# Splitting one layer's ConvFFN weights ahead of time, during the attention layer before it

## The chip, the cores and the metric

The kernel runs on one core of a Trainium2 chip, in one launch. The metric is the device time of that launch in microseconds (us). The names used below are those of the profile: PE (TensorE matmuls), PEld (its weight loads), DVE (VectorE), ACT (ScalarE), POOL (GpSimd), SP (SyncE, which issues the DMAs).

## What is computed

One step of a decoder trunk of two layers, on 1,024 prompt tokens and 8 sample tokens (1,032 columns, model width 1,024), everything in float32. Layer 0 is *even*: its mixer is windowed attention beside an RWKV-7 recurrence, joined by an output projection. Layer 1 is *odd* (gated spatial mixing). Each layer ends in a ConvFFN of width 2,816, which is the part that the change is about:

```python
def conv_ffn(xn, conv_state, w_gate, w_up, conv_w, conv_b, w_down):
    ...
    gpre = xn @ w_gate
    ext = jnp.concatenate([conv_state.astype(gpre.dtype), gpre], axis=1)
    conv = conv_b + conv_w[CONV_W - 1] * ext[:, CONV_W - 1:CONV_W - 1 + t]
    ...
    h = jax.nn.gelu(conv, approximate=True) * (xn @ w_up)
```

followed by `h @ w_down`, a norm and the residual.

## The kernel before

**Products in three passes.** TensorE multiplies in a format with fewer mantissa bits than float32. So each operand is split into a high part (the value rounded to that format) and a low part (what is left), and a product is three matmuls: high by high (L290), high by low (L291), low by high (L292). `split` (L285 to L287) makes the two parts: ACT copies the high one (L286), then POOL or DVE subtracts it from the source (L287).

**Weights.** Weights come in slabs of 128 output columns, 1,024 rows deep. A list `order` holds all uses in the order of the program; `wget` (L274) hands out the next, and before that calls `wload` (L229) for the slabs up to a look-ahead: 1 slab in the even layer, 3 in the ConvFFN's plain part (`LOOK`, `LOOK2`). `wload` treats a slab as two halves of 128 x 512 (256 KB). A half that is seen for the first time is loaded raw (L260) and split; if the same slab is used again later, its two parts are also stored to DRAM (`wk`, L264), and every later use loads those two parts (L255, twice 256 KB) and splits nothing. Gate and up slabs of the ConvFFN (names that begin with `ga` or `up`) are left out of that: each use loads them raw and splits them anew. All these DMAs are issued on SP.

**The even layer (layer 0)** works on four chunks of tokens (256, 256, 256, 264). For each chunk c, proj(c) runs 20 slabs `win_even` and out(c) runs 8 slabs `wout_even`; in between stands core(c), attention and the RWKV chunk recurrence, with many short dependent steps. The stages come in the order proj(0), proj(1), proj(2), out(0), proj(3), out(1), out(2), out(3). In the trace proj(2), out(0), proj(3) and most of out(1) lie between 236 and 600 us. A projection's columns that RWKV needs pass through `lerp` (L914): the last column of the chunk before is copied into `zm` by POOL (L927), ACT fills the rest (L928), POOL copies the new last column into `carry` (L930), and DVE mixes (L931). Slabs of the even layer accumulate in two PSUM banks called `le`.

**The sample tokens** go through their own chain in the even layer: `attn_sample` (from L1156; its first ACT step after the scores is L1189), then `rwkv_sample` (from L1225): some small matmuls, two transposes (L1269), a trip of the rows through DRAM, four rounds on the matrix state (L1292 to L1302, POOL and DVE), a second trip through DRAM, and the transpose L1311. After it the ConvFFN's operand tiles `xA` are filled and its first slabs run.

**A small ring.** `stile` (L141) hands out tiles from a ring of four buffers, tag `s`. Norm inputs, residuals, the sample chain's tiles (`Vc`, `st`, `pr`, `spT`, `stmp`, `rows`, `S`, `St`) and the ConvFFN's input loads `xl` (L522) all come from it, so whoever asks for a tile waits for the release of the one four requests back.

**The first ConvFFN.** Its tokens are two halves, A (512) and B (520). Ten columns of blocks f = 0 to 9 are *plain*: gate slab f and up slab f, first for A, then for B (20 slabs, each used twice: 80 half-slab loads and 80 splits). out(2) and out(3) of the even layer still run in between A's first slabs. Then 12 blocks follow in pairs with a seven-product scheme, whose token combinations DVE prepares (L589 to L620) while B starts; then `w_down`. In the trace A starts at about 718 us, B at about 880 to 910, and the pairs at about 1001.

The scheduler fixes each engine's order when the program is built; on the chip an engine runs its list in that order and waits where an operand isn't ready.

Of the kernel before, what the change touches and what calls it, by code (L numbers as in the profile page):

```python
# [10 lines left out]
F32R = mybir.dt.float32r  # L11
# [5 lines left out]
P = 128  # L17
# [106 lines left out]
def trunk(ctx: ExitStack, tc: tile.TileContext, A, O):  # L124
    nc = tc.nc
    PE, ACT, DVE, POOL, SP = nc.tensor, nc.scalar, nc.vector, nc.gpsimd, nc.sync
# [10 lines left out]
    def nm(s):  # L137
        uid[0] += 1
        return f"{s}_{uid[0]}"
# [18 lines left out]
    def dram(shape, s, dt=F32):  # L158
        return dp.tile(shape, dt, tag=s, name=s)
# [17 lines left out]
    order = []  # L177
# [19 lines left out]
    wcount, wmore, wkept = [0], [], {}  # L197
    wfirst = next(i for i, o in enumerate(order) if o[0] == "gate0")

    def wtile(late):  # L200
        if late:
            wcount[0] += 1
        if late and (wcount[0] <= 4 * W2ONLY or wcount[0] % (NW + FBUFS["w2"]) >= NW):
            return wmore[0]("w2", 512, F32R)
        return wp.tile([P, 512], F32R, tag="w", name=nm("w"))
# [3 lines left out]
    def wfactor(name, f, i):  # L209

        if i == 0:
            wraw[name, f] = [stile("wa")[:, 0:512] for _ in range(4)]
            for k, t in enumerate(wraw[name, f]):
                SP.dma_start(out=t, in_=A[name][f + k // 2][:, k % 2 * 512:k % 2 * 512 + 512])
        r = wraw[name, f]
        if i == 0:
            return r[0]
        if i == 1:
            r.append(stile("ws", "g")[:, 0:512])
            DVE.tensor_tensor(out=r[4], in0=r[2], in1=r[3], op=ALU.add)  # L220
            return r[4]
        if i == 2:
            DVE.tensor_tensor(out=r[4], in0=r[4], in1=r[0], op=ALU.subtract)
            return r[4]
        if i == 3:
            return r[1]
        if i == 4:
            DVE.tensor_tensor(out=r[2], in0=r[0], in1=r[2], op=ALU.subtract)
            return r[2]  # L229
        if i == 5:  # L230
            DVE.tensor_tensor(out=r[4], in0=r[1], in1=r[4], op=ALU.subtract)
            return r[4]
        return r[3]

    def wload(i):

        late = i >= wfirst
        if late:  # L240
            look[0] = LOOK3 if len(order[i]) == 3 else LOOK2
        if len(order[i]) == 3:
            hi, lo = wtile(late), wtile(late)
            split(wfactor(*order[i]), hi, lo, POOL)
            wtiles[i] = tuple([x[:, k * P:(k + 1) * P] for k in range(4)] for x in (hi, lo))
            return
        name, m = order[i]
        again = name[:2] not in ("ga", "up") and order.index((name, m)) < i
        more = name[:2] not in ("ga", "up") and order.count((name, m)) > 1
        hi, lo = [], []  # L250
        for j in range(2):
            t = [wtile(late) for _ in range(2)]
            if again:
                for part in range(2):
                    SP.dma_start(out=t[part].bitcast(F32), in_=wkept[name, m, j, part])  # L255
                hi.append(t[0])
                lo.append(t[1])
                continue
            raw = wp.tile([P, 512], F32, tag="raw", name=nm("raw"), bufs=NRAW)
            SP.dma_start(out=raw, in_=A[name][m][:, j * 512:j * 512 + 512])  # L260
            split(raw, *t, DVE if SW[0] <= i - wfirst < SW[1] and i % SW[2] == 0 or i < SW[3] else POOL)
            for part in range(2 if more else 0):
                kept = wkept[name, m, j, part] = dram([P, 512], nm("wk"))
                SP.dma_start(out=kept, in_=t[part].bitcast(F32))  # L264
            hi.append(t[0])
            lo.append(t[1])
        wtiles[i] = ([hi[k // 4][:, (k % 4) * P:(k % 4 + 1) * P] for k in range(KD)],
                     [lo[k // 4][:, (k % 4) * P:(k % 4 + 1) * P] for k in range(KD)])

    wpos = [0]  # L270

    def soon():

# [2 lines left out]
    def wget(*key):  # L276
        i = wpos[0]
        wpos[0] += 1
        assert order[i] == key, (order[i], key)
        while wnext[0] <= min(i + look[0], len(order) - 1):  # L280
            wload(wnext[0])
            wnext[0] += 1
        return wtiles.pop(i)

    def split(src, hi, lo, eng=None):  # L285
        ACT.activation(out=hi, in_=src, func=AF.Copy)  # L286
        (eng or DVE).tensor_tensor(out=lo, in0=src, in1=hi.bitcast(F32), op=ALU.subtract)  # L287
# [528 lines left out]
def even_layer(env, bnd):  # L816
    g = NSpace(env)
    tc, nc, A, O = g.tc, g.nc, g.A, g.O
    PE, ACT, DVE, POOL, SP = g.PE, g.ACT, g.DVE, g.POOL, g.SP
    SE = [DVE if x == 'd' else POOL for x in SENG]  # L820
    bank, C, V, stile = g.bank, g.C, g.V, g.stile
# [8 lines left out]
    def et(s, n, dt=F32):  # L830
        return (eb if s in LASTING else ec).tile([P, n], dt, tag=s, name=g.nm(s), bufs=EB.get(s, 1))

    def pt_(s):
        return et("p", 528)


    lora = const.tile([P, 512], F32, tag="lora", name="lora")
# [988 lines left out]
```

## Time and profile before

| what | value |
|---|---|
| time, three runs | 2580.53, 2581.8 (median), 2583.38 us |
| the profiled execution | 2581.03 us; its span, first to last instruction, 2579.3 us |
| mean granted TensorE clock | 0.968 of full speed |
| PE, DVE, ACT, POOL busy | 95%, 65%, 39%, 36% of the span |
| HBM | 341.34 MB read, 153.64 MB written, 192 GB/s over the span |
| POOL, splits of weights (L287, 300 of `raw`) | 427.2 us |
| ACT, high parts of weights (L286, 320 of `raw`) | 199.2 us |

PE is the engine with the most work, so a change pays where PE idles, or where it runs at a lower granted clock after idling. The table's busy shares are means over stages with different limits; what matters here are two stretches, the even layer's third and fourth chunk (236 to 600 us, and on to 718) and the up phase of the first ConvFFN (718 to 1001 us).

### The profile page before, as it was taken

What the parts mean: (1) busy time and instruction counts of PE and PEld (TensorE: products, weight loads), DVE (VectorE), ACT (ScalarE), POOL (GpSimd) and SP (SyncE); (2) the same over time, 40 slices, a digit from 0 to 9 for tenths busy, and PEclk for the clock granted to TensorE, in tenths of its full rate; (3) what the DMA queues carried; (4) which work ended last, traced back from release to release, by engine and by line L of the source; (5) the groups of instructions that cost most, each with busy time, mean ns of one, the idle gap of its engine ahead of it and who ended that gap; (6) DMA issues with size and microseconds to landing.
All of it is one profiled execution on the core that took longest, in us unless ns stands there. A gap on an engine that the chain in (4) does not pass through costs nothing. (4 is left out here: it accounts for less than half of the span.)

```text
span 2579.3 us, 49838 instructions
## 1 busy us (share of the span) xinstructions
PE 2447.2 (95%) x18460; PEld 2259.5 (88%) x18460; DVE 1670.7 (65%) x3581; ACT 1003.0 (39%) x1979; POOL 939.2 (36%) x981
## 2 busy tenths in 40 slices
PE   6789998999899899999999999999979999999996
PEld 5678988888788799999998888999879999998985
DVE  5776849756874846666455776435896766655556
ACT  4453545434354344444301143343534444441110
POOL 1611113110455645555323253032655555542221
PEclk9999999999799899999999999999989999999998
DMA  8876757765486743323646888465664233254585
GB/s 314 274 240 208 226 179 236 239 221 164 155 272 217 244 152 99 123 83 123 220 148 228 299 280 277 148 234 197 214 210 140 98 105 123 84 208 148 183 290 167
DMA packets 307603, 500.92 MB, mean 194 GB/s; under 512 B 50272, under 2 KB 93856, under 8 KB 307360
## 3 DMA queue, kind: packets, MB, share of 16 engines
q1 hardware_dynamic: 307360, 497.75, 58.3%
q8 instruction: 145, 2.38, 0.4%
q14 instruction: 98, 0.80, 0.1%
HBM read 341.34 MB, written 153.64 MB: 192 GB/s over the span
## 5 line engine op out<-in xcount | busy, mean ns | idle before, releaser
L287 POOL TENSOR_TENSOR w<-raw,w 128x512 fp32r<-128x512 f32 x300 | 427.2, 1432 | 664.5 <-ACT w L286 602.0
L286 ACT ACTIVATE w<-raw 128x512 fp32r<-128x512 f32 x320 | 199.2, 629 | 478.8 <-PE l L291 296.3
L290 PE MATMUL l<-xB,w 128*128 128x256 f32 (+2 forms) x1120 | 320.0, 286 | 17.9 <-DVE gb L589 16.2
L291 PE MATMUL l<-xB,w 128*128 128x256 f32 (+2 forms) x1120 | 320.5, 286 | 5.1 <-DVE xB L287 5.1
L292 PE MATMUL l<-xB,w 128*128 128x256 f32 (+2 forms) x1120 | 320.5, 286 | 0.0
L291 PE MATMUL l<-xA,w 128*128 128x512 f32 (+1 forms) x896 | 305.9, 341 | 0.0
L290 PE MATMUL l<-xA,w 128*128 128x512 f32 (+1 forms) x896 | 304.6, 341 | 0.5 <-DVE ob L1342 0.3
L292 PE MATMUL l<-xA,w 128*128 128x512 f32 (+1 forms) x896 | 304.9, 340 | 0.0
L290 PE MATMUL le<-xs,w 128*128 128x256 f32 (+1 forms) x896 | 269.9, 302 | 25.4 <-ACT w L286 17.9
L292 PE MATMUL le<-xs,w 128*128 128x256 f32 (+1 forms) x896 | 268.1, 300 | 7.4 <-POOL w L287 5.8
L291 PE MATMUL le<-xs,w 128*128 128x256 f32 (+1 forms) x896 | 264.6, 296 | 0.7 <-DVE xs L287 0.7
L290 PEld LDWEIGHTS l<-xB,w 128*128 128x128 f32 x1120 | 214.3, 192 | 18.6 <-DVE gb L589 16.6
L291 PEld LDWEIGHTS l<-xB,w 128*128 128x128 f32 x1120 | 214.6, 192 | 5.5 <-DVE xB L287 5.3
L292 PEld LDWEIGHTS l<-xB,w 128*128 128x128 f32 x1120 | 214.5, 192 | 0.1
L290 PEld LDWEIGHTS le<-xs,w 128*128 128x128 f32 x896 | 177.9, 199 | 38.9 <-ACT w L286 21.2
L287 POOL TENSOR_TENSOR w<-wa,w 128x512 fp32r<-128x512 f32 x112 | 178.1, 1596 | 57.7 <-ACT w L286 57.7
L730 DVE TENSOR_TENSOR yA<-yA,l 128x512 f32<-128x512 f32 x160 | 110.1, 688 | 132.7 <-PE l L292 131.6
L292 PEld LDWEIGHTS le<-xs,w 128*128 128x128 f32 x896 | 177.1, 198 | 15.5 <-POOL w L287 7.4
L290 PEld LDWEIGHTS l<-xA,w 128*128 128x128 f32 x896 | 169.6, 189 | 19.5 <-ACT w L286 0.6
L292 PEld LDWEIGHTS l<-xA,w 128*128 128x128 f32 x896 | 169.6, 189 | 18.9 <-issue 0.2
L291 PEld LDWEIGHTS l<-xA,w 128*128 128x128 f32 x896 | 169.4, 189 | 18.9 <-DVE pp L311 0.3
L291 PEld LDWEIGHTS le<-xs,w 128*128 128x128 f32 x896 | 178.0, 199 | 4.3 <-issue 2.1
(484 smaller groups left out, 6532.7 us busy)
## 6 DMA issues: line engine op xcount, KB each, us to landing
w<-wk SPq DMA_DIRECT2D x496, 256.0 KB, 4.0
wk<-w SPq DMA_DIRECT2D x272, 256.0 KB, 3.7
raw<-in_down_dram SPq DMA_DIRECT2D x88, 256.0 KB, 4.6
ta<-hd SPq DMA_DIRECT2D x36, 512.0 KB, 4.6
raw<-in_gate_dram SPq DMA_DIRECT2D x64, 256.0 KB, 3.1
raw<-in_up_dram SPq DMA_DIRECT2D x64, 256.0 KB, 3.0
hd<-cb SPq DMA_DIRECT2D x28, 516.0 KB, 3.9
hd<-ub SPq DMA_DIRECT2D x28, 516.0 KB, 3.9
```

Of the source, the lines that this page charges most:

```text
L286: ACT.activation(out=hi, in_=src, func=AF.Copy)
L287: (eng or DVE).tensor_tensor(out=lo, in0=src, in1=hi.bitcast(F32), op=ALU.subtract)
L290: PE.matmul(out, wh, xh, start=start, stop=False, **kw)
L291: PE.matmul(out, wh, xl, start=False, stop=False, **kw)
L292: return PE.matmul(out, wl, xh, start=False, stop=stop, **kw)
L730: DVE.tensor_tensor(out=yc, in0=yc, in1=ps[:, :n], op=ALU.add)
```

## The change

The 20 plain slabs of the first ConvFFN are loaded and split once, ahead of time. A generator `ahead` walks over their 40 halves; `wget` advances it by one half at each of the 40 slabs `win_even` of proj(2) and proj(3) (20 each), so that all 40 halves are done by it. For one half: SP loads the raw half into a tile `ar` of the ring `s`; ACT copies the high part into `ah` (one buffer); POOL subtracts in place, so that `ar` then holds the low part; ACT's queue issues the store of the high part and POOL's queue the store of the low part. `wload` finds these halves in `wkept`, so each of the 80 half-slab uses in the first ConvFFN loads two parts (L255's line) and splits nothing. Lines after the inserted ones move by 16 (helpers) or 18 (even layer).

```diff
--- before.py
+++ after.py
@@ -245,8 +245,8 @@
             wtiles[i] = tuple([x[:, k * P:(k + 1) * P] for k in range(4)] for x in (hi, lo))
             return
         name, m = order[i]
-        again = name[:2] not in ("ga", "up") and order.index((name, m)) < i
-        more = name[:2] not in ("ga", "up") and order.count((name, m)) > 1
+        again = (name, m, 0, 0) in wkept
+        more = name[:2] not in ("ga", "up") and not again and order.count((name, m)) > 1
         hi, lo = [], []
         for j in range(2):
             t = [wtile(late) for _ in range(2)]
@@ -267,7 +267,21 @@
         wtiles[i] = ([hi[k // 4][:, (k % 4) * P:(k % 4 + 1) * P] for k in range(KD)],
                      [lo[k // 4][:, (k % 4) * P:(k % 4 + 1) * P] for k in range(KD)])
 
-    wpos = [0]
+    def ahead(keys):
+
+        for name, m in keys:
+            for j in range(2):
+                raw, hi = stile("ar")[:, 0:512], room[0]()
+                SP.dma_start(out=raw, in_=A[name][m][:, j * 512:j * 512 + 512])
+                split(raw, hi.bitcast(F32R), raw.bitcast(F32R), POOL)
+                for part, (eng, t) in enumerate(((ACT, hi), (POOL, raw))):
+                    kept = wkept[name, m, j, part] = dram([P, 512], nm("wk"))
+                    eng.dma_start(out=kept, in_=t)
+                yield
+
+    wpos, room = [0], [None]
+    first_ffn = dict.fromkeys(o for o in order if o[0] in ("gate0", "up0") and len(o) == 2)
+    spare = ahead(first_ffn)
 
     def soon():
 
@@ -280,6 +294,8 @@
         while wnext[0] <= min(i + look[0], len(order) - 1):
             wload(wnext[0])
             wnext[0] += 1
+        if key[0] == "win_even" and i >= order.index(("wout_even", 0)) - 20:
+            next(spare, None)
         return wtiles.pop(i)
 
     def split(src, hi, lo, eng=None):
@@ -832,6 +848,8 @@
 
     def pt_(s):
         return et("p", 528)
+
+    g.room[0] = lambda: et("ah", 512)
 
 
     lora = const.tile([P, 512], F32, tag="lora", name="lora")
```

How the engines' orders move, at three places on which the prediction rests:

POOL, in the fourth chunk's projection (`carry` and `zm` are the copies of `lerp`; the memsets belong to the RWKV chunk). Before:

```order
L930 COPY carry_4413<-zm_4450 128x1
L927 COPY zm_4528<-carry_2438 128x1
L1414 MEMSET uv_3455 64x512
L1413 MEMSET uv_3543 64x512
L930 COPY carry_4413<-zm_4490 128x1
L927 COPY zm_4567<-carry_2438 128x1
L1423 MEMSET iv_3465 64x256
L1424 MEMSET iv_3465 64x16
L1423 MEMSET iv_3561 64x256
L1424 MEMSET iv_3561 64x16
```

Now:

```order
L303 TENSOR_TENSOR ar_4425<-ar_4425,ah_4426 128x512
L948 COPY carry_4413<-zm_4508 128x1
L279 DMA wk_4432<-ar_4425 128x512
L945 COPY zm_4603<-carry_2438 128x1
L1441 MEMSET iv_3465 64x256
L1442 MEMSET iv_3465 64x16
L948 COPY carry_4413<-zm_4555 128x1
L1441 MEMSET iv_3561 64x256
L303 TENSOR_TENSOR ar_4474<-ar_4474,ah_4475 128x512
L1442 MEMSET iv_3561 64x16
L945 COPY zm_4650<-carry_2438 128x1
L279 DMA wk_4481<-ar_4474 128x512
```

Between the copies there now stand a subtraction of a half (`ar<-ar,ah`) and the issue of its store on POOL itself (`DMA wk<-ar`).

ACT, around the sample tokens' first step, `st<-pp` (`y<-le` closes a slab of out(1), `at`, `es`, `pT`, `oa` are attention, `Z`, `nW` the recurrence). Before:

```order
L1107 ACTIVATE qx_8721<-q_7212 64x256 x2
L324 ACTIVATE p_9304<-y_9029 128x512
L1189 ACTIVATE st_7869<-pp_7860 128x64
L1145 ACTIVATE pT_8438<-m_8439 128x512
L1198 ACTIVATE pr_7874,sq_1479_7875<-pr_7874,sq_1479_7875 64x136
L1200 ACTIVATE sq_1479_7875<-vec,sq_1479_7875 64x1
L1404 ACTIVATE bkt_8206<-pr_8201 128x512
L1153 ACTIVATE oa_7831<-m_8445 128x128
L1590 ACTIVATE y_9029<-le_9107 128x256
```

Now:

```order
L302 ACTIVATE ah_8104<-ar_8103 128x512
L1608 ACTIVATE y_9390<-le_9603 128x256
L1499 ACTIVATE Z_8635<-ch_8680 32x256
L279 DMA wk_8108<-ah_8104 128x512
L1505 ACTIVATE nW_8677<-ch_8699 32x8x32
L1163 ACTIVATE pT_9257<-m_9258 128x512
L302 ACTIVATE ah_8148<-ar_8147 128x512
L1522 ACTIVATE Z_8734<-ch_8721 64x512
L1505 ACTIVATE nW_8677<-ch_8700 32x8x32
L279 DMA wk_8152<-ah_8148 128x512
L1171 ACTIVATE oa_8191<-m_9264 128x128
L1608 ACTIVATE y_9390<-le_9637 128x256
L1207 ACTIVATE st_8229<-pp_8220 128x64
```

`st` stood ahead of out(1)'s third `y`; now it follows out(1)'s last one, behind the last two high parts `ah` and their stores.

PE, at the end of the sample tokens' rows (`pp<-cst,smp` is L1269, L1287 after the change; `le<-xs,w` are slabs of the output projection, `ch` the recurrence of the fourth chunk, `m` attention). Before:

```order
L291 MATMUL le_9277<-xs_119,w_9239 128x256
L292 MATMUL le_9277<-xs_117,w_9240 128x256
L1269 MATMUL pp_7987<-cst,smp 128x128
L1506 MATMUL ch_8361<-Z_8374,nW_8317 64x64 x8
L1144 MATMUL m_8740<-cst,at_8717 128x128 x4
L1269 MATMUL pp_7992<-cst,smp 64x128
L1513 MATMUL ch_8385<-uv_8112,bkt_8110 64x64 x8
```

Now:

```order
L1279 MATMUL pp_8343<-stmp_8300,cst 128x32
L1524 MATMUL ch_9027<-Z_9040,nW_8984 64x64 x8
L1287 MATMUL pp_8347<-cst,smp 128x128
L1531 MATMUL ch_9051<-uv_8568,bkt_8566 64x64 x8
L1533 MATMUL ch_9027<-uv_8568,Am_8527 64x64 x4
L1287 MATMUL pp_8352<-cst,smp 64x128
L1533 MATMUL ch_9027<-uv_8568,Am_8527 64x64 x4
L1351 MATMUL ch_9169<-cst,ot_8720 128x128 x4
```

Before, the two transposes stood inside and right behind out(1)'s last slab, with more attention and three more groups of the recurrence still to come; now out(1) and all of the attention lie ahead of them, and only the end of the recurrence and out(2) follow before L1311.

## Rows read from the trace of the kernel before

**Rows 1.** The page's section 1: the span, and each engine's busy time, share of the span and instructions.

```profile
span 2579.3 us, 49838 instructions
PE 2447.2 (95%) x18460; PEld 2259.5 (88%) x18460; DVE 1670.7 (65%) x3581; ACT 1003.0 (39%) x1979; POOL 939.2 (36%) x981
```

**Rows 2.** The table by stretches of the first ConvFFN's A half and the start of its B half. Columns: from:to and length in us; then busy time (and instructions) of PE, PEld, DVE, ACT and POOL; the granted TensorE clock as a share of 2.4 GHz; the mean busy share of the 16 DMA engines; GB/s moved.

```profile
720.00:830.00 110.00, 110.00 (x593) 93.85 (x593) 69.00 (x128) 54.34 (x101) 56.78 (x73) 1.00 0.74 241
830.00:840.00 10.00, 6.39 (x28) 4.84 (x26) 8.75 (x8) 4.70 (x10) 10.00 (x9) 1.00 0.60 206
840.00:850.00 10.00, 9.96 (x33) 8.14 (x34) 6.30 (x16) 3.65 (x6) 5.11 (x5) 0.66 0.41 129
850.00:860.00 10.00, 10.00 (x46) 7.94 (x45) 6.25 (x13) 4.23 (x7) 5.29 (x6) 1.00 0.83 258
860.00:870.00 10.00, 10.00 (x48) 8.20 (x47) 7.46 (x15) 5.15 (x9) 3.26 (x4) 1.00 1.05 371
870.00:880.00 10.00, 10.00 (x85) 10.00 (x85) 10.00 (x15) 5.13 (x10) 7.70 (x3) 1.00 0.83 312
880.00:890.00 10.00, 4.90 (x32) 4.70 (x31) 10.00 (x12) 2.80 (x7) 5.57 (x4) 0.72 0.66 185
890.00:900.00 10.00, 9.46 (x73) 9.25 (x72) 9.14 (x11) 3.39 (x7) 9.96 (x7) 0.94 0.62 204
900.00:910.00 10.00, 2.93 (x13) 2.93 (x14) 8.68 (x15) 2.91 (x7) 2.83 (x2) 0.58 0.83 261
```

**Rows 3.** The view of waits from 720 to 960 us: engine and line that waited, what it waited for, us in total, times, longest.

```profile
PE l L290 <- DVE gb L589: 7.6, 1, 7.6
...
PE l L291 <- DVE xB L287: 5.1, 1, 5.1
...
PE pp L332 <- DVE sq L330: 3.7, 1, 3.7
```

**Rows 4.** The time order of DVE's instructions: start us, duration us, then line, operation, tiles, shapes and count.

```profile
882.33 3.43 DVE L596 TENSOR_TENSOR yB<-t,yB 128x516 fp32r<-128x516 f32 x2
...
888.72 0.68 DVE L620 TENSOR_TENSOR xc<-xc,ub 128x516 f32<-128x516 f32 x1
...
896.44 1.78 DVE L620 TENSOR_TENSOR xc<-xc,ub 128x516 f32<-128x516 f32 x1
...
898.14 0.68 DVE L596 TENSOR_TENSOR yB<-t,yB 128x516 fp32r<-128x516 f32 x1
```

**Rows 5.** The time order of POOL's instructions in the same stretch, in the same columns.

```profile
873.61 11.60 POOL L287 TENSOR_TENSOR w<-raw,w 128x512 fp32r<-128x512 f32 x4
...
894.49 3.18 POOL L287 TENSOR_TENSOR w<-raw,w 128x512 fp32r<-128x512 f32 x2
```

**Rows 6.** Groups by line from 720 to 1000 us (the up phase of the first ConvFFN): the splits of weights. After the count: busy time, mean ns of one, then the idle time before them and what ended it.

```profile
L287 POOL TENSOR_TENSOR w<-raw,w 128x512 fp32r<-128x512 f32 x76 | 115.2, 1522 | 93.8 <-ACT w L286 86.6 <-DMA w<-wk 6.8
...
L286 ACT ACTIVATE w<-raw 128x512 fp32r<-128x512 f32 x77 | 48.3, 629 | 56.5 <-PE l L291 32.5 <-DMA raw<-in_up_dram 9.2 <-DMA raw<-in_gate_dram 8.6
```

**Rows 7.** The table by stretches again (columns as in Rows 2): the even layer's third and fourth chunk, and the stretch around the start of the ConvFFN.

```profile
236.00:600.00 364.00, 350.59 (x3263) 314.85 (x3262) 261.76 (x864) 170.72 (x419) 71.99 (x137) 0.95 0.68 215
700.00:840.00 140.00, 134.93 (x780) 115.76 (x779) 89.93 (x162) 66.63 (x127) 71.68 (x88) 1.00 0.75 248
```

**Rows 8.** DMA issues from 700 to 840 us: tiles, queue, count, KB each, median us from issue to landing.

```profile
raw<-in_up_dram SPq DMA_DIRECT2D x19, 256.0 KB, 3.0
raw<-in_gate_dram SPq DMA_DIRECT2D x19, 256.0 KB, 3.3
```

**Rows 9.** Groups by line from 236 to 600 us, columns as in Rows 6.

```profile
L287 POOL TENSOR_TENSOR w<-raw,w 128x512 fp32r<-128x512 f32 x16 | 21.7, 1359 | 44.8 <-ACT w L286 27.4 <-DMA w<-wk 11.6 <-DMA ivd<-Am 5.6
...
L927 POOL COPY zm<-carry 128x1 f32<-128x1 f32 x26 | 6.3, 241 | 74.8 <-DVE p L931 37.6 <-DVE wd L931 18.0 <-DVE zv L931 12.1
```

**Rows 10.** One line's instructions, L255 (SyncE's loads of kept weight parts) from 236 to 600 us: durations in ns of an issue, least/median/greatest.

```profile
L255 SPq DMA_DIRECT2D w<-wk x184: 319/382/1392, 236.1 to 599.7; - x184
```

**Rows 11.** The page's section 6, the stores of weight parts, in the same columns as Rows 8.

```profile
wk<-w SPq DMA_DIRECT2D x272, 256.0 KB, 3.7
```

**Rows 12.** The time order (columns as in Rows 4) of the sample tokens' chain on ACT, PE, POOL, and PE again.

```profile
589.93 0.21 ACT L1189 ACTIVATE st<-pp 128x64 f32<-128x64 f32 x1
...
639.73 0.27 PE L1269 MATMUL pp<-cst,smp 128*64 128x128 f32 x1
...
656.09 1.26 POOL L1292 TENSOR_TENSOR St<-S,rows 128x512 f32<-128x512 f32 x1 [2.61 <-DMA S<-in_wkv_state_dram]
...
667.65 1.27 POOL L1299 TENSOR_TENSOR S<-S,St 128x512 f32<-128x512 f32 x1
...
697.19 1.28 POOL L1292 TENSOR_TENSOR St<-S,rows 128x512 f32<-128x512 f32 x1 [1.53 <-DVE ov L1302]
...
702.37 1.27 POOL L1299 TENSOR_TENSOR S<-S,St 128x512 f32<-128x512 f32 x1
...
717.82 0.24 PE L1311 MATMUL pp<-cst,orow 32*128 32x32 f32 x1
```

**Rows 13.** The table by stretches (columns as in Rows 2) from the last step ahead of the sample tokens' state rounds to their end.

```profile
640.00:654.00 14.00, 13.18 (x171) 11.18 (x170) 10.86 (x39) 8.98 (x24) 4.26 (x4) 1.00 0.41 119
654.00:690.00 36.00, 28.29 (x240) 24.39 (x239) 33.34 (x83) 13.40 (x35) 15.79 (x12) 0.57 0.43 134
690.00:716.00 26.00, 25.22 (x232) 23.65 (x231) 15.73 (x33) 6.65 (x16) 7.89 (x11) 1.00 0.80 272
```

## The prediction

> **What bounds the kernel now.** The page's table of engines comes first: PE is busy 2447.2 us of a span of 2579.3 [rows 1], so only stretches in which PE stands still, or runs at a lower granted clock, can give anything back. I looked for those in the first ConvFFN, where the splits go away, by the table of stretches [rows 2]. From 720 to 830 us PE is busy 110.00 of 110.00 at full clock: the splits cost nothing there. It idles 3.61 us at 830 to 840, 5.10 at 880 to 890, 0.54 at 890 to 900 and 7.07 at 900 to 910, 16.3 in all. The clock adds to it: at 840 to 850 it is 0.66 and 33 matmuls run where 46 run in the next slice, (46 - 33) / 46 x 10 = 2.8 us; busy time by missing clock gives 4.90 x 0.28 + 9.46 x 0.06 + 2.93 x 0.42 = 3.2 more. The whole stake is 16.3 + 6.0 = 22.3 us.
>
> The view of waits names what ends the idle time: DVE's multiplication of a gate (7.6 us), its split of B's input (5.1), its sum of squares (3.7) [rows 3]. None of the three is a weight. What a weight's split has to do with them is seen in time order. DVE's L620 takes 1.78 us at 896.44 and 0.68 at 888.72, and two L596 take 3.43 at 882.33 where one takes 0.68 at 898.14 [rows 4]; POOL subtracts weight parts from 873.61 to 885.21 and from 894.49 to 897.67, over the slow ones [rows 5]. So POOL's splits slow DVE, which at 870 to 890 is busy 20.00 of 20.00 and holds up B's start.
>
> **The ConvFFN: what goes.** In the up phase POOL spends 115.2 us on 76 subtractions and ACT 48.3 on 77 copies [rows 6]. With the 80 plain ones nearly all of it goes, at most the whole stake of 22.3 us: PE is full elsewhere. Two things stay. DVE still has all the combinations to make; about 1.1 us per slow instruction is what it gets back. And the weights get heavier: a half was one raw load of 256 KB, now it is two. From 700 to 840 us there are 19 + 19 raw loads [rows 8], so 38 x 0.262 = 10.0 MB more on 248 GB/s x 140 us = 34.7 MB [rows 7]. That makes 319 GB/s, and a DMA share of 0.75 x 319 / 248 = 0.96. The best slice shows 371 GB/s at 1.05 [rows 2]. It fits, with no room for a burst, in a stretch where PE loses nothing now. SP has 80 more issues of 0.38 us [rows 10], 31 us over the 283 of the up phase, and hides them. I take **-14** for this part, two thirds of the stake for the fuller transfers, between -22.3 (everything comes back) and 0 (late weights eat what DVE returns).
>
> The Trainium skill ("HBM Reference", section "Specifications (TRN2)") says that a core streaming alone gets about 425 GB/s, more than its paired share of 358. By that figure 319 GB/s would leave a quarter free and this term would be nearer -18; no slice here shows more than 371, so I keep to the row.
>
> **The even layer: what comes.** Forty halves, from about 236 us on. *ACT*: 40 copies of 0.629 us [rows 6] and 40 store issues of about 0.38 [rows 10] are 40 us, beside 170.72 busy of 364 [rows 7]; it hides them. But there is one `ah`: a copy waits on ACT until the store before it has landed, 3.7 us for such a store [rows 11]. Behind it in ACT's order stand the copies that empty the two `le` banks, and PE waits for those. Halves are asked for one per slab, and 364 us / 40 is 9 us apart, more than 0.6 + 0.4 + 3.7 = 4.7, so I cost this at nothing; where halves bunch it is up to 4 us each time. *POOL*: 40 subtractions of 1.36 to 1.52 us [rows 6, 9] are 54 to 61 us. The trace has no DMA issued by POOL; the nearest row is SP's issue, 0.32 to 1.39 us [rows 10], so 13 to 56 us more; I take 15, by the median. POOL is busy 71.99 of 364 and stays below half. The copies into `zm`, 0.24 us each and idle 74.8 us ahead of them now [rows 9], have that much room. *DVE*: 261.76 of 364 busy, 0.72. If each subtraction hits one DVE instruction as above, that is 40 x 1.1 x 0.72 = 32 us of DVE time; PE waits for little of it, as it is busy 350.59 of 364 [rows 7]. *DMA*: 40 x (0.262 read + 0.524 written) = 31.5 MB, 86 GB/s on top of 215, so a share of 0.68 x 301 / 215 = 0.95 with one slab of look-ahead. That is the part that I fear: a slab that lands late stops PE at once. I take **+6** for the layer's body, 0.3 us for each of the 20 slabs of the fuller half of it; the ends are 0 and +32 (all of DVE's loss).
>
> The Trainium skill ("SBUF — State Buffer", section "A bandwidth-pool intuition that's wrong (but worth ruling out)") states that a DMA issued on GpSimd, 620 ns alone, takes 3100 ns beside a DVE copy, since its descriptors wait for DVE. By that rule POOL's 40 stores would take 124 us instead of 15, the ring would give its tiles back later, and I would double the term to +12. No row here shows such a DMA.
>
> **The sample tokens: what is moved.** `ar` comes from the ring of four that the sample chain uses too, and in the new order the chain's first step stands behind the last two halves and behind out(1)'s last slab. Now that step runs at 589.93 us, the last transpose at 639.73, the state rounds from 656.09, and PE takes L1311 at 717.82, with A's first slab right behind it [rows 12]. From transpose to L1311 are 78.1 us. PE's own work in them, at full clock, is 13.18 + 28.29 x 0.57 + 25.22 = 54.5 us [rows 13]. In the new order only what now runs from about 684 us stays behind the transposes: 25.22 and about 3, 28 us. So 54.5 - 28 = 26.5 us of work moves ahead of the chain's slow part, which then runs with less beside it. If the chain takes as long as before, A starts 26.5 us later. It may run faster: the last round, with DVE less loaded, takes 702.37 + 1.27 - 697.19 = 6.5 us to its state, the first 667.65 + 1.27 - 656.09 = 12.8, so three rounds can gain up to 19. I take two thirds of that, **+13**; the ends are +26.5 (nothing gained) and +7.5 (all of it).
>
> **The sum.** -14 + 6 + 13 = +5 on the profiled execution's 2581.0 gives 2586.0; that execution lies 0.8 below the median of 2581.8, so 2586.8, **2587 us**. About 0.2%, 5.2 us, is what a measurement of this kernel can tell from no change: the forecast lies on that edge.
>
> **Rivals.** *Forecast* (0.44): the even layer's costs eat the ConvFFN's gain and a little more; by its own terms from 2579 (18 returned, +2 and +13) to 2599 (14 returned, +6 and +25). For it: the DMA shares of 0.95 and 0.96, and PE's order.
>
> *Faster* (0.38): the sample chain, freed of the competition of attention on DVE, gains back all of the 19 (+7), the early weights land in time (+2), and the ConvFFN returns 18: 2581.8 - 9 = 2573. For it: PE waits for weights hardly anywhere now, POOL is busy a fifth of the time in the even layer, and DVE at 654 to 690 is busy 33.34 of 36.00 [rows 13], the competition that would go. Against it: the chain's four rounds and two trips through DRAM depend on each other.
>
> *Much slower* (0.10): the chain through the ring. If the last halves, waiting for ring tiles, `ah` and stores, come after out(1)'s last slab by their own chain (14 pairs stand back to back on POOL; at 4.7 us a pair that is 66 us), `st` waits with them; if half of the 66 lies behind out(1), A starts 33 us later: 2581.8 + 6 + 33 - 14 = 2607. It decides once the last half's store lands later than out(1)'s end, 638 us now.
>
> *Transfer-bound A half* (0.08): the DMA share reaches 1 in 700 to 840, slabs land late, PE idles at its half clock after. Were 290 GB/s all that it sustains, 319 / 290 would stretch the 116 us up to 836 by 12, and of 14 returned 2 were left: 2581.8 + 19 - 2 = 2599.
>
> That the splits don't move is no rival: 40 calls of the right kind meet 40 halves, and the orders show all of them.
>
> **Chances and range.** Faster by over 0.2%: 0.38, the second case. Within: 0.17, the forecast's part from 2579 to 2587. Slower: 0.27 + 0.10 + 0.08 = 0.45. The range takes in the faster case down to 2566 (22.3 returned, less 7) and the slower up to 2606, which leaves out the far end of the ring's case.
>
> **What would show it.** ConvFFN right: no `w<-raw` split before 1000 us, DVE's L596 and L620 near 0.68, and PE idle at B's start below 6 us. Even layer right: DMA share over 0.9 in proj(2) and proj(3), and waits of `le` for `w<-wk` of 5 us in sum. Sample right: L1311 (now L1329) over 10 us later relative to out(1)'s last slab, with PE idle or at half clock in out(2). The forecast is wrong if A starts within 5 us of 718, or if the slabs of A wait for `w<-wk`.

## The result and the profile after

The change makes the kernel slower: 2615.7 us in the median of four runs (2607.19 to 2618.95), against 2581.16 (four runs beside it); the ratio is 1.0121 [1.0102, 1.0140]. The profiled execution took 2607.19 us, the fastest of the four, so the rows below explain 26 us of the 34.5. The forecast was 2587, the range ended at 2606.

The page's first section, and the two new DMA queues of its third (ACT's stores, then POOL's: packets, MB, share of 16 engines), against [rows 1]:

```profile
span 2605.4 us, 50065 instructions
PE 2456.4 (94%) x18460; PEld 2267.4 (87%) x18460; DVE 1652.7 (63%) x3577; ACT 978.7 (38%) x1939; POOL 896.2 (34%) x985
...
q10 hardware_dynamic: 5760, 10.49, 1.1%
q0 software_dynamic: 3200, 10.49, 1.0%
```

PE works about as long (9 us more) in a span that is 26.1 us longer. Three places on the way show where the time goes. `xA`'s first result comes at 740.5 us before and 789.1 after (+48.6). B's last plain gate or up result comes at 996.4 and 1028.2 (+31.8). The end is at +26.1. So 48.6 us are lost ahead of the ConvFFN, 16.8 come back in its up phase, and 5.7 more after it. These last 5.7 can't be put down to the change: the part behind B's last plain result runs the same program in all twenty kernels of this document and takes 1575.8 to 1588.3 us in their traces.

**The loss.** The time order of POOL, ACT, SP, PE and POOL (columns as in [rows 4]), to be read against [rows 12]:

```profile
651.36 1.26 POOL L303 TENSOR_TENSOR ar<-ar,ah 128x512 fp32r<-128x512 f32 x1 [5.29 <-ACT ah L302]
...
652.35 0.36 ACT L1608 ACTIVATE y<-le 128x256 f32<-128x256 f32 x1
...
652.61 0.20 ACT L1207 ACTIVATE st<-pp 128x64 f32<-128x64 f32 x1
...
653.13 1.02 SPq L1338 DMA_DIRECT2D bon<-bd  x1
...
695.94 0.34 SPq L1290 DMA_DIRECT2D rows_d<-rr  x1
...
697.57 0.42 PE L1287 MATMUL pp<-cst,smp 128*64 128x128 f32 x1
...
713.13 1.45 POOL L1310 TENSOR_TENSOR St<-S,rows 128x512 f32<-128x512 f32 x1
...
722.37 1.27 POOL L1317 TENSOR_TENSOR S<-S,St 128x512 f32<-128x512 f32 x1
...
748.27 1.27 POOL L1310 TENSOR_TENSOR St<-S,rows 128x512 f32<-128x512 f32 x1 [1.52 <-DMA w<-wk]
...
753.43 1.30 POOL L1317 TENSOR_TENSOR S<-S,St 128x512 f32<-128x512 f32 x1
```

The last half is subtracted at 651.36. `st`, the sample chain's first step, runs at 652.61 where it ran at 589.93, right behind out(1)'s last `y`. The last transpose is at 697.57 (639.73), the first state round at 713.13 (656.09), and L1329, which was L1311 at 717.82, runs at 769.5:

```profile
L1329 PE MATMUL pp<-cst,orow x1: 243/243/243, 769.5 to 769.5; 32*128 32x32 f32 x1
```

The table by stretches, columns as in [rows 2], against [rows 13] and [rows 2]:

```profile
640.00:654.00 14.00, 11.63 (x134) 9.58 (x134) 3.55 (x9) 6.61 (x19) 5.12 (x6) 0.99 0.85 273
654.00:670.00 16.00, 15.60 (x178) 13.82 (x179) 5.16 (x22) 7.09 (x21) 0.51 (x1) 0.82 0.33 111
670.00:685.00 15.00, 15.00 (x146) 14.24 (x143) 10.39 (x40) 3.25 (x13) 0.43 (x2) 0.50 0.00 1
685.00:700.00 15.00, 14.61 (x119) 12.09 (x116) 2.24 (x7) 3.68 (x9) 0.00 (x0) 0.50 0.03 9
700.00:715.00 15.00, 9.76 (x87) 8.14 (x85) 11.15 (x26) 6.16 (x12) 8.17 (x7) 0.84 0.35 98
715.00:730.00 15.00, 4.20 (x18) 3.78 (x18) 13.47 (x38) 2.13 (x5) 6.51 (x6) 0.54 0.28 96
730.00:740.00 10.00, 5.74 (x30) 5.53 (x31) 7.67 (x15) 2.52 (x4) 5.46 (x7) 0.66 0.67 215
740.00:750.00 10.00, 4.84 (x31) 4.46 (x30) 4.56 (x7) 0.77 (x2) 6.52 (x6) 0.79 0.93 291
750.00:760.00 10.00, 9.70 (x65) 8.91 (x63) 3.48 (x5) 1.04 (x3) 3.24 (x3) 0.87 1.05 388
790.00:915.00 125.00, 125.00 (x651) 105.89 (x650) 65.12 (x148) 39.08 (x68) 14.83 (x28) 1.00 0.93 314
750.00:890.00 140.00, 137.47 (x755) 117.87 (x754) 65.16 (x153) 43.81 (x83) 20.31 (x50) 0.99 0.94 320
```

In [rows 13] only 654 to 690 us was near half clock (0.57). Now the clock is 0.50 from 670 to 700, and PE is busy 4.20 of 15.00 us at 715 to 730. The transfers stop altogether at 670 to 685: a DMA share of 0.00. SP stands before the sample rows' first store, in its own order:

```profile
SPq L1290 <- ACT rr L1289: 38.8, 2, 38.6
```

That wait of 38.6 us is seen in the order of time above as the gap from 653.13 to 695.94. Behind it on SP stand the loads for out(2) and the tiles of the state rounds; PE then waits for the loads (`le <- w` 6.2 us between 650 and 790). The same wait, of 38.6 to 43.6 us, is in the five traces in which stored halves hold the ring of four right up to `st` (the change, e3, e11, e17 and e18 below); in the other fifteen it is at most 3.1 us at a time. No run took it away alone, so what it costs is not shown.

**The return.** From 790 to 915 PE is busy 125.00 of 125.00. Two rows answer [rows 3] and [rows 4]: the longest wait that is left in the up phase, and DVE's L596 and L620, now L612 and L636:

```profile
PE l L306 <- DVE gb L605: 3.1, 1, 3.1
```

```profile
922.55 1.30 DVE L612 TENSOR_TENSOR yB<-t,yB 128x516 fp32r<-128x516 f32 x2
...
937.28 0.68 DVE L636 TENSOR_TENSOR xc<-xc,ub 128x516 f32<-128x516 f32 x1
```

The three waits of 7.6, 5.1 and 3.7 us have become one of 3.1 (two more are 0.3 and 0.2), and each instruction takes 0.65 to 0.68 us with no split of POOL's over it. The return is steady. With the same 168 matmuls of the even layer's output projection (`le<-xs`) left to run in it, the stretch from A's first to B's last plain result takes 238.7 to 239.2 us in the four kernels that load split parts (the change, e11, e17, e18), and 248.9 to 255.9 us in six that split raw slabs there (before, e3, e6, e13, e14, e15), so it is worth 10 to 17 us.

### The profile page after: what moved, and what is told of

It is laid out like the page before. It is cut to its first block, busy times and chain, and to the rows that moved or that the text cites. A ratio compares the mean times of both kernels' runs of the same rounds, so it can differ in the third digit from the quotient of the medians.

```text
span 2605.4 us, 50065 instructions
## 1 busy us (share of the span) xinstructions
PE 2456.4 (94%) x18460; PEld 2267.4 (87%) x18460; DVE 1652.7 (63%) x3577; ACT 978.7 (38%) x1939; POOL 896.2 (34%) x985
## 5 line engine op out<-in xcount | busy, mean ns | idle before, releaser
L303 POOL TENSOR_TENSOR w<-raw,w 128x512 fp32r<-128x512 f32 x224 | 311.0, 1398 | 547.7 <-ACT w L302 510.3
L302 ACT ACTIVATE w<-raw 128x512 fp32r<-128x512 f32 x240 | 149.3, 629 | 413.4 <-PE l L307 266.7
L306 PE MATMUL le<-xs,w 128*128 128x256 f32 (+1 forms) x896 | 274.2, 307 | 31.1 <-ACT w L302 15.9
L308 PE MATMUL le<-xs,w 128*128 128x256 f32 (+1 forms) x896 | 271.8, 304 | 11.1 <-POOL w L303 6.4
L307 PE MATMUL le<-xs,w 128*128 128x256 f32 (+1 forms) x896 | 266.1, 297 | 2.9 <-DVE xs L303 2.9
L306 PEld LDWEIGHTS le<-xs,w 128*128 128x128 f32 x896 | 180.5, 202 | 46.0 <-ACT w L302 19.2
L308 PEld LDWEIGHTS le<-xs,w 128*128 128x128 f32 x896 | 180.0, 201 | 20.1 <-POOL w L303 8.8
L307 PEld LDWEIGHTS le<-xs,w 128*128 128x128 f32 x896 | 180.9, 202 | 5.5 <-DVE xs L303 3.1
```

What stands on the lines that cost most here:

```text
L306: PE.matmul(out, wh, xh, start=start, stop=False, **kw)
L307: PE.matmul(out, wh, xl, start=False, stop=False, **kw)
L308: return PE.matmul(out, wl, xh, start=False, stop=stop, **kw)
```

## The experiments

Eighteen kernels ran. A ratio is to the kernel before, run beside it on the same chip, where its median was 2581.2 to 2589.0 us; so it is not the quotient of two medians of a table. Where the ConvFFN runs on raw slabs, the split halves are made and not read. Line numbers are those of each kernel.

**First theory: the ring delays the sample chain, and A waits for it. Rival: the halves' work and bytes slow the even layer.**

e1, `ar` from the buffers of raw weights instead of the ring:

```diff
-                raw, hi = stile("ar")[:, 0:512], room[0]()
+                raw, hi = wp.tile([P, 512], F32, tag="raw", name=nm("ar"), bufs=NRAW), room[0]()
```

> The raw tiles of the split-ahead halves come from the three buffers that raw weights use, not from the ring of four that the sample tokens' chain uses; all else as in the change. Theory 1 (the ring moved the sample chain behind the last halves, and A waits for it): A starts within 10 us of 718 + what the even layer's body costs (up to 14), the ConvFFN's gain of 17 stays, so 2566 to 2580 us. Theory 2 (the 40 splits and their 31.5 MB slow the even layer, wherever their tiles are): 2605 us or more, as the change.

e2, the halves one chunk earlier:

```diff
-        if key[0] == "win_even" and i >= order.index(("wout_even", 0)) - 20:
+        if key[0] == "win_even" and i >= order.index(("wout_even", 0)) - 40:
```

> The change with the halves taken one chunk earlier: in proj(1) and proj(2) instead of proj(2) and proj(3). The ring is the same, but the last half is done before the sample chain begins. Theory 1: the chain starts near 590 to 610 us again, A near 720 to 735, total 2568 to 2582 us. Theory 2: the same splits and bytes are in the even layer, 2600 us or more.

e3, the split parts not used:

```diff
-        again = (name, m, 0, 0) in wkept
+        again = name[:2] not in ("ga", "up") and (name, m, 0, 0) in wkept
```

> The change, with all 40 halves split and stored ahead, but the ConvFFN loads and splits its raw slabs as before, so nothing is returned there. Theory 1: the even layer's loss alone: A starts near 766 us as in the change, the ConvFFN takes what it took before: 2581 + 48 = 2629 us, give or take 6. Rival to the ConvFFN's gain (its heavier loads cost what the missing splits return): no slower than the change, 2607 to 2617 us.

e4, both edits of e1 and e3.

> As the first run (raw tiles from the raw-weight buffers), and the ConvFFN loads and splits its raw slabs as before. Theory 1: only the body's cost of 40 splits and 31.5 MB is left, 2583 to 2597 us; its distance to the first run is the ConvFFN's gain, 13 to 22 us. Theory 2: 2620 us or more.

| kernel | median us | ratio | `st` at, us | first A result, us |
|---|---|---|---|---|
| before | 2581.2 | 1 | 589.9 | 740.5 |
| change | 2615.7 | 1.0121 [1.0102, 1.0140] | 652.6 | 789.1 |
| e1 | 2603.0 | 1.0075 [1.0049, 1.0100] | 616.4 | 764.9 |
| e2 | 2602.3 | 1.0067 [1.0041, 1.0094] | 635.6 | 793.0 |
| e3 | 2626.8 | 1.0170 [1.0141, 1.0200] | 654.7 | 794.2 |
| e4 | 2607.7 | 1.0098 [1.0066, 1.0131] | 615.8 | 768.6 |

Out of the ring the chain starts 36 us earlier, and the ratio falls by 0.0046 (12 us). That is less than an order alone can move (the fourth part), so how much of the loss is the ring's is not shown by it. Most of the loss stays, so the first theory falls as the whole cause. In e2 the loss only moves: out(0)'s first result is already 43.5 us late. e3 against the change, 0.0049 or 13 us, fits the ConvFFN's return, and the even layer's own loss is then 44 us. e4 against e1 returns only 6 (the intervals overlap). A's column is not level: when A's first result comes, 11 of the 32 results of the output projection (`y<-le`) are still to come in e1 and 10 in e4, but 8 in the others. e2 and e3 lie where one theory put them (the second and the first), e1 and e4 between the two.

**Second: which part of the halves costs?** All on e4's base but e8.

e5, 8 columns of 512 in every load, copy, subtraction and store (the slices of the load and the size of `wk` likewise):

```diff
-                raw, hi = wp.tile([P, 512], F32, tag="raw", name=nm("ar"), bufs=NRAW), room[0]()
+                raw, hi = (x[:, 0:8] for x in (wp.tile([P, 512], F32, tag="raw", name=nm("ar"), bufs=NRAW), room[0]()))
```

> As e4 (raw tiles from the raw-weight buffers, the ConvFFN on raw slabs), but each ahead step handles 8 columns of the 512: the same 40 loads, copies, subtractions and 80 stores at the same places of the program, with 1/64 of the bytes and columns of short instructions. Theory 2 (the bytes and the engines' work cost the even layer): 2582 to 2590 us. Theory 3 (the steps, however small, make the scheduler put PE's, ACT's and DVE's instructions into another order, with less independent work between dependent steps): 2596 us or more, as e4.

e6, no stores:

```diff
-                for part, (eng, t) in enumerate(((ACT, hi), (POOL, raw))):
-                    kept = wkept[name, m, j, part] = dram([P, 512], nm("wk"))
-                    eng.dma_start(out=kept, in_=t)
```

> As e4, with the 40 loads, copies and subtractions, but none of the 80 stores (21 MB less). Theory 2, if the written bytes or the single tile that waits for them count most: 2582 to 2592 us. Theory 2, if ACT's and POOL's work counts most, or theory 3: 2598 us or more.

e7, no copy and no subtraction, and so no tile `ah`:

```diff
-                raw, hi = wp.tile([P, 512], F32, tag="raw", name=nm("ar"), bufs=NRAW), room[0]()
+                raw, hi = wp.tile([P, 512], F32, tag="raw", name=nm("ar"), bufs=NRAW), None
...
-                split(raw, hi.bitcast(F32R), raw.bitcast(F32R), POOL)
-                for part, (eng, t) in enumerate(((ACT, hi), (POOL, raw))):
+                for part, eng in enumerate((ACT, POOL)):
...
-                    eng.dma_start(out=kept, in_=t)
+                    eng.dma_start(out=kept, in_=raw)
```

> As e4, with the 40 loads and 80 stores (both store the raw half), but no copy on ACT and no subtraction on POOL. Theory 2, if the transfers count: 2598 us or more; if ACT's and POOL's work counts: 2582 to 2592 us. Theory 3: 2596 us or more.

e8, on e1's base, lower priority for the scheduler:

```diff
+                with tc.high_priority(offset=-600):
```

> As e1 (raw tiles from the raw-weight buffers, the ConvFFN uses the split parts), with the ahead steps at a lower priority by 600 when the scheduler makes the order, so that other ready work goes first. Theory 3: the order of the rest comes nearer to the old one, 2575 to 2592 us. Theory 2: the same bytes and work, 2598 to 2610 us.

e5 gives 2604.8 us, 1.0084 [1.0055, 1.0113]; e6 2582.3, 0.9991 [0.9973, 1.0010]; e7 2611.8, 1.0105 [1.0063, 1.0146]; e8 2589.7, 1.0020 [1.0005, 1.0036]. So the bytes are not it: with 1/64 of them the loss is the same as in e4. Loads, copies and subtractions at full size cost nothing that can be measured in e6. The kernels that store lose, with the bytes or without. What a store does here apart from moving bytes is to hold its tile until it lands, and to wait in its queue; and with it in the program the scheduler writes another order. ACT's view of waits from 100 to 760 us, first e5, then e6 (us in total, times, longest):

```profile
ACT ah L302 <- DMA wk<-ah: 36.2, 16, 4.6
```

```profile
ACT ah L299 <- POOL ar L300: 17.6, 13, 4.1
```

In e5 16 of the 40 copies wait for the store before them, in e6 13 wait for POOL's subtraction. That fits, but doesn't settle it: in e4, with a ratio no better than e5's, the same wait is 11.0 us. And e7 has no `ah` at all and loses as much (1.0105), so the wait for that one buffer isn't needed for the loss. All four runs lie in a range that was written for them: e5, e7 and e8 in the third theory's (e7's is also that of the transfers), e6 in the one for stores that cost.

**Third: is it the queue that issues the stores?**

e9 is e4, and e10 is e1, with this edit; e11 is the change with it alone; e12 is e4 with `(ACT, hi), (SP, raw)`:

```diff
-                for part, (eng, t) in enumerate(((ACT, hi), (POOL, raw))):
+                for part, (eng, t) in enumerate(((SP, hi), (SP, raw))):
```

> As e4 (raw tiles from the raw-weight buffers, the ConvFFN on raw slabs), but all 80 stores are issued on SP, none on ACT or POOL. Theory 4 (a store issued on ACT or POOL waits there in order, for its data, its tile or an earlier transfer, and holds up the short dependent steps behind it): 2580 to 2589 us, as without stores. Theory 2 in the form that is left (any store of these bytes costs): 2598 us or more. Theory 3 (any new order costs): 2596 or more.

> As e1 (raw-weight buffers, the ConvFFN uses the split parts), stores issued on SP. Theories 1 and 4 together: nothing of the even layer's loss is left and the ConvFFN's gain of 6 to 17 shows: 2564 to 2577 us. Against them: 2590 us or more.

> The change with one edit: the stores are issued on SP. The tiles still come from the sample chain's ring, and that chain's first step still follows out(1)'s last slab in the order. Theories 1 and 4: the body's loss goes, the chain's stays (25 to 35 us), the ConvFFN returns 15: 2590 to 2603 us. If theory 4 alone holds: 2564 to 2577. If theory 1 alone: 2607 to 2617.

> As e9, but the high parts' stores are on ACT's queue again, the low parts' on SP. Theory 4, ACT's part: if ACT's in-order waits are the larger part of the loss, 2594 us or more; if POOL's are, 2580 to 2589.

e9 gives 2620.6 us, 1.0135 [1.0100, 1.0169]; e10 2621.0, 1.0147 [1.0105, 1.0189]; e11 2626.2, 1.0162 [1.0139, 1.0185]; e12 2597.4, 1.0051 [1.0034, 1.0068]. Theory 4 falls: off ACT and POOL the stores cost no less (e10 and e11 are slower than e1 and the change; the intervals of e9 and e4 overlap). SP issues every load of weights, and now two stores per half stand ahead of those loads. From 230 to 680 us in e9, SP waits 9.9 us at these stores for copies and subtractions; whether that is their cost was not tested. The lowest of the three splits is e12's, in the range for ACT's part. e11 lies above all three of its ranges.

**Fourth: the new order itself, or the stores?** Every edit makes the scheduler write other lists.

e13 is the change without stores (the edits of e3 and e6 on the ring of four); e14 is e6 with e2's edit. e15 and e16 are the kernel before, and e17 and e18 the change, with one number of the line `with tc.high_priority(offset=1000):` ahead of a chunk's input norm (L1594 before), which sets how early the scheduler takes that norm:

```diff
-        with tc.high_priority(offset=1000):
+        with tc.high_priority(offset=500):
```

(500 in e15 and e17, 1400 in e16 and e18.)

> The change without its 80 stores: loads, copies and subtractions in the ring of four, one chunk as in the change; the ConvFFN on raw slabs. In this order the sample chain's first step stands behind out(1)'s first slab again. Theory 5 (the stores hold the tiles until they land): 2580 to 2590 us. Theory 3 (any new order costs): 2598 us or more. Theory 1 in its plain form (any use of the ring by the halves delays the sample chain): 2600 us or more.

> As e6 (raw-weight buffers, no stores, the ConvFFN on raw slabs) one chunk earlier, in proj(1) and proj(2): a third order without stores. Theory 5: 2580 to 2590 us. Theory 3: 2598 us or more.

> The kernel before with nothing added: the priority that brings a chunk's input norm forward in the scheduler is 500 instead of 1000, which moves some 1,300 of the first 6,400 rows of PE's order. Theory 5: 2578 to 2590 us. Theory 3: 2596 us or more.

> The same with 1400 instead of 1000, which moves some 2,750 of the first 6,400 rows of PE's order, about as many as the change. Theory 5: 2578 to 2590 us. Theory 3: 2596 us or more.

> The whole change on top of e15 (norm priority 500). If the change's loss is its own (the stores hold the tiles, and the sample chain stands behind out(1) in this order too), it is again 20 to 45 us against e15's 2562, so 2580 to 2605. If it was an accident of one order, 2545 to 2570.

> The whole change on top of e16 (norm priority 1400). If the loss is the change's own, 20 to 45 us against e16's 2578: 2598 to 2622. If it was an accident of one order, 2560 to 2588.

For each profiled execution the table splits the span: PE idle is the span less PE's busy time; the clock's part is the busy time by what is missing of the span's mean clock; the rest is PE's work at full clock. That mean takes in the low clock of idle time, so the clock's part comes out 10 to 20 us too large, and the work as much too small: over PE's busy records alone the part is 60.0 before, 66.9 in the change, 83.4 in e5, 62.3 in e6 and 49.6 in e15.

| kernel | median us | ratio | PE idle | clock | work |
|---|---|---|---|---|---|
| before | 2581.2 | 1 | 132.1 | 78.3 | 2368.9 |
| change | 2615.7 | 1.0121 [1.0102, 1.0140] | 149.0 | 86.0 | 2370.4 |
| e5, small stores | 2604.8 | 1.0084 [1.0055, 1.0113] | 136.1 | 96.4 | 2374.8 |
| e6, no stores | 2582.3 | 0.9991 [0.9973, 1.0010] | 129.9 | 78.5 | 2373.4 |
| e13, no stores, ring | 2568.6 | 0.9947 [0.9928, 0.9967] | 121.0 | 73.5 | 2375.8 |
| e14, no stores, early | 2590.5 | 1.0045 [1.0019, 1.0070] | 130.2 | 76.2 | 2382.0 |
| e15, before, 500 | 2561.6 | 0.9919 [0.9892, 0.9946] | 120.4 | 65.8 | 2373.0 |
| e16, before, 1400 | 2577.7 | 0.9970 [0.9952, 0.9988] | 124.3 | 81.1 | 2377.6 |
| e17, change, 500 | 2620.9 | 1.0136 [1.0095, 1.0176] | 153.0 | 91.1 | 2371.8 |
| e18, change, 1400 | 2623.2 | 1.0135 [1.0102, 1.0168] | 150.2 | 96.4 | 2374.6 |

Theory 3 holds in half: an order alone is worth up to 22 us, and here to the faster side, so single differences below that say little (e8, e12 and e14 among them). Of theory 5, that stores cost holds for the class; that they do it by the tiles that they hold is not shown. Without stores three orders stand at 0.9947, 0.9991 and 1.0045; with the whole change three orders stand at 1.0121, 1.0135 and 1.0136, 1.2 to 2.2% above the kernel with the same number and without the change. All the other kernels with stores are slower than the one before as well, from 1.0020 (e8) to 1.0170 (e3). e8 has the ConvFFN's return in it; among the kernels that split raw slabs, those with stores stand at 1.0051 (e12) to 1.0170, so the two groups only just part at e14 and e12. The times went past many of the ranges: e13, e15 and e16 are faster than any that was written for them, e14 lies at its edge, and e17 and e18 are slower than theirs.

The clearest pair is e3 and e13, whose programs differ in the 80 stores alone (1.0170 and 0.9947, 58 us). The copies of the halves, first in e3, then in e13 (ns of one, then first and last start in us):

```profile
L302 ACT ACTIVATE ah<-ar x40: 614/629/647, 270.5 to 652.7; 128x512 fp32r<-128x512 f32 x40
```

```profile
L299 ACT ACTIVATE ah<-ar x40: 614/629/645, 272.3 to 562.1; 128x512 fp32r<-128x512 f32 x40
```

With the stores the last half comes 90 us later, and in e3, as in the change, `st` comes behind it, at 654.7. In these runs the ring harms only where stores hold its tiles: the sample chain's first step on ACT, first in e13, then in e17:

```profile
593.21 0.20 ACT L1204 ACTIVATE st<-pp 128x64 f32<-128x64 f32 x1
```

```profile
668.91 0.22 ACT L1207 ACTIVATE st<-pp 128x64 f32<-128x64 f32 x1
```

With the halves in the ring but no stores the step runs at 593.21, as before; with stores and e15's number at 668.91. What stays open is how a store costs the even layer its 20 us in e4 and e5, where the ring is out of it: the held tiles (the raw ones alone would do, by e7), the store's place in its queue, and the order that the scheduler writes for a program with stores were not told apart. More buffers were not tried.

e15, one number and no added work, is the fastest kernel of the study, faster than both; its clock beside e5's in the view of spans:

```profile
core 0: 2559.2 us, clock 0.973
```

```profile
core 0: 2607.3 us, clock 0.961
```

## Why the prediction was wrong

**What held.** PE bounds the kernel, and its work at full clock hardly differs between the kernels (2368.9 and 2370.4). The ConvFFN's term was -14: the profile has 16.8 less from A's first to B's last plain result, e3 against the change 13. DVE's slow instructions are gone, as was said. The heavier transfers were worked out as 319 GB/s at a share of 0.96 over the 140 us around A's start; in the stretch that answers to it, 750 to 890, they are 320 at 0.94, and PE waits for none of A's slabs. So the rival of a transfer-bound A half did not come true. The Trainium skill ("HBM Reference", section "Specifications (TRN2)") gives about 425 GB/s for a core that streams alone; the 388 of 750 to 760 lies below that, and shows that my 371 was no ceiling.

**The step that failed is "The sample tokens: what is moved",** which took +13 with an upper end of +26.5. The mechanism came as forecast: `st` stands behind the last halves and out(1)'s last slab, and A starts late. The size was wrong. L1329 comes 51.7 us later than L1311. By the prediction's own terms this has three parts. Out(1)'s last `y` is 14.2 us later (638.16 to 652.35); the even layer's body was taken at +6. From there to the last transpose it takes 45.2 us where it took 1.6: 43.6 more, where I had 26.5. From the transpose to L1329 it takes 71.9 instead of 78.1 us, so the chain gained 6.2 where I took 13. So the term that I took at +13 measured 43.6 - 6.2 = 37.4.

What I left out is the chain's first half. By [rows 12] it takes 49.8 us from `st` (589.93) to the last transpose (639.73), and nearly all of it ran beside out(1), whose eight results come from 584.7 to 638.2 (five of them after 600; that most of out(1) lies before 600, as said at the start, is wrong). When `st` moves behind out(1), this half moves behind it as well, and I gave it no term: I measured from the transposes, and let them wait for PE's work alone. Counted from `st`, the account is simple: `st` is 62.7 us later, the first half takes 45.0 instead of 49.8, the second 71.9 instead of 78.1, and 62.7 - 4.8 - 6.2 = 51.7. In all twenty traces the first half takes 40.0 to 54.5 us.

There is a second reading. This stretch of the change, then the first half of the chain in e17 and in e16, columns as in [rows 2]:

```profile
652.35:697.57 45.22, 44.42 (x437) 39.32 (x435) 17.01 (x67) 15.07 (x46) 1.77 (x5) 0.63 0.15 48
```

```profile
668.91:708.92 40.01, 38.34 (x363) 34.34 (x364) 13.77 (x54) 10.41 (x34) 2.89 (x5) 0.62 0.05 16
```

```profile
596.05:637.84 41.79, 41.40 (x456) 38.35 (x453) 28.51 (x137) 20.07 (x66) 0.49 (x2) 0.96 0.63 188
```

PE is busy for 44.42 of the 45.22 us, and at a clock of 0.63 that is 28 us of work at full clock. So my 26.5 us was about the right amount of work, and priced at the granted clock it would have come near the 43.6 (26.5 / 0.63 = 42). But in e16 the half takes as long at a clock of 0.96, with more work beside it, as in e17 at 0.62. How much of the 45 us is the chain's own steps, and how much their waiting for PE at the lower clock, stays open.

**What I did not see** is SP. I hid its issues by their number. A store that waits for its data stands in SP's order too, and the sample rows' store held it for 38.6 us, the DMA share at 0.00 from 670 to 685.

**The even layer's body.** I feared the bytes, at a share of 0.95. From 236 to 600 us the share was 0.84, and from 236 to 640 PE's `le` waited 4.0 us for `w<-wk` (0.8 before): late slabs make up little of the 14.2. What grew most is attention's wait for DVE, 11.8 us in two groups against 2.3 before (`m` for `mx` and `at`, L1144):

```profile
PE m L1162 <- DVE mx L1142: 7.6, 5, 2.4
PE m L1162 <- DVE at L1157: 4.2, 1, 4.2
```

Why DVE is late there was not tested. e5 shows that the bytes are not what costs, e6 that ACT's and POOL's work is not either, and e7 that the one buffer `ah`, which I costed at nothing, isn't needed for the loss. The stores on POOL took 0.557 us each to issue (I took 0.38), and ACT's 0.327:

```profile
L279 ACTq DMA_DIRECT2D wk<-ah x40: 326/327/355, 275.4 to 651.3; - x40
L279 POOL DMA_DIRECT2D wk<-ar x40: 557/557/728, 277.2 to 652.9; - x40
```

The Trainium skill ("SBUF — State Buffer", section "A bandwidth-pool intuition that's wrong (but worth ruling out)") gives 3100 ns for a DMA that GpSimd issues beside a DVE copy. No issue here took over 0.728 us, and from issue to landing the median is 5.2 us for POOL's stores and 4.9 for ACT's. No row here shows whether DVE ran such a copy at those moments, so the rule is neither shown nor refuted, but the term of 124 us that I worked out from it is not there.

**The rivals.** "Much slower" (0.10) named the place and the kind: last halves behind out(1)'s end, `st` behind them, 2607 us. In the profiled execution the time was that to 0.2 us, but by another sum (51.7 lost and more returned than it took). So the match is luck. "Faster" rested on the chain making up its shift; behind the transposes it made up 6 us.

## What to carry to other kernels

Work that is free by its engines' busy shares can still cost a layer of short dependent steps. Here the loss went with the 80 stores, and not with their bytes or with the copies and subtractions; look at who next asks for the buffers that a store holds, and at what stands behind it in its queue. When a step moves, measure from the first step of its chain that moves, not from a later one. Where a scheduler writes the order, run an unrelated reordering of the same kernel as a control before a difference of 1% is put down to an edit: here one number moved 22 us.

## What was not expected of the hardware

In all these kernels PE's work at full clock is 2367 to 2383 us by the table's method (2386 to 2399 over PE's busy records), while the spans go from 2559.2 to 2631.4. So nearly all of what they differ by is idle time and lower clock. The two needn't go together: in e5 the clock's part grew by 18 us (23 over the busy records) while PE's idle time grew by 4. Why it grew there was not tested.
